# Output projection by seven products: another order of the products, product 1 in one part, weight loads spread over the tokens' terms

## The chip, the cores and the metric

The kernel runs on one core of a Trainium2 chip. The metric is the time of one execution on the device, in microseconds (us). A run is timed three times and the median is given. One more execution is taken by the hardware profiler; all rows below come from that one.

## The reference, cut to what matters

One block: a mixer (neighbourhood attention for half of the channels, a long convolution called Hyena for the other half), an output projection with a residual, then a mixture of 16 experts. The change is in the output projection only.

```python
mixed = jnp.concatenate([group_rms_norm(attn, attn_out_g[i], N_ATTN_HEADS),
                         group_rms_norm(hy, hyena_out_g[i], N_HYENA_GROUPS)], axis=-1)
x = x + jnp.einsum('bsd,de->bse', mixed, w_out[i])      # 1024 x 2048 by 2048 x 2048, float32
x = x + expert_choice_moe(rms_norm(x, ffn_norm_g[i]), w_router[i], w_gate[i], w_up[i], w_down[i])
```

## The kernel before, in words

**Stages.** The kernel first computes the input projection (tiles `pj`), woven with attention heads 0 to 5 and the filters, then the Hyena groups, then heads 6 and 7 (`attention`), then the output projection (`out_stream`, accumulators `o`), then for each token tile the router (`route`), then the top-k on VectorE and the experts (`pa`).

**Precision.** A float32 factor is split into a rounded part and a rest (`split`, L60 on ScalarE and L61 on VectorE; `wh` and `wl` for weights). One product of 128 x 128 by 128 x 512 is three matmuls (`mm3`, L68): rounded by rounded, rounded by rest, rest by rounded. The stationary operand is a piece of `s` (mixed tokens), the moving one is `wh` or `wl`.

**Seven products.** The projection is cut in halves three ways: tokens (512 each), channels (attention, Hyena) and columns. By the scheme of Strassen and Winograd, four blocks of the result come from seven products instead of eight. This is done twice, for `n` = 0 and 1, each with 2 x 512 columns. In `out_stream`, `where` names the four blocks of `w_out`: "11" and "12" belong to the attention channels, "21" and "22" to the Hyena channels. Each block is four loads of 512 KB (`load`, DRAM to tiles `b`). The sums of blocks are formed on VectorE (L943, L940, L946, L1015), and the generator `pairs` splits them; `wh` and `wl` have five buffers, and a product uses four of each. Products 2 and 4 need only Hyena outputs, product 1 only attention outputs, the others sums of both.

**Tokens' side.** `store_mixed` writes, for each head or group, rounded part and rest (`mxh`, `mxl`, one buffer each) of its combinations into seven DRAM arrays `sd`, one per product (L757): a head of the last two (6 and 7) writes five pairs, in the order 1, 5, 7, 6, 3. `fetch` reads 128 tokens of one array at a time, 1 MB, into `s` (two buffers).

**Jobs.** A job is one product and one quarter `t` of its 512 tokens: 8 channel blocks by 3 matmuls, 24 matmuls into one PSUM bank, in four parts `q` of 6. Before the change the order of products is 2, 1, 6, 4, 7, 5, 3. For `n` = 0 product 1 is cut in two: part 0 takes channel blocks 0 to 5 (heads 0 to 5), part 1 takes blocks 6 and 7 after both heads are mixed (the `yield lambda` on `self.mixed`). The four banks `o` stay open between them.

**What sets the order.** `weave` deals out generators by a modelled clock, so parts `q` fall between the pieces of head 7. A scheduler then fixes one order of instructions for each engine; engines work through it strictly in order, and SyncE (SP) issues nearly all DMAs from one such list. A DMA that has to wait therefore holds all DMAs behind it.

**Head 7.** For each of its eight query tiles j: scores `a` on TensorE, bias and maximum (`pe`, `ast`) on VectorE, exponential on ScalarE (L855), four or five transposes `t<-ident,pe`, a copy `pT` on ScalarE, and the product with the values (`t<-raw,pT`). Before tile 2, the second half of queries and keys is normalized (`raw`, L733) and transposed (`t<-ident,raw`).

Of the kernel before, what the change touches and what calls it, by code (L numbers as in the profile page):

```python
# [37 lines left out]
class Block:  # L38
# [862 lines left out]
    def out_stream(self, ctx):  # L901
# [12 lines left out]
        units = [(n, i) for n in range(2) for i in (2, 1, 6, 4, 7, 5, 3)]  # L914
# [3 lines left out]
        def load(n, name):  # L918
            c, k = where[name]
            B[n, name] = []  # L920
            for q in range(4):
                w = mp.tile([P, 2, 512], F32, name="b" + name, bufs=4)
                nc.sync.dma_start(w, a["w_out"][c + n, k + q])
                B[n, name].append(w)
# [8 lines left out]
        def pairs():  # L933
            for n, i in units:
                for q in range(4):
                    def b(x):
                        return B[n, x][q]

                    if i == 4:
                        tt(b("21"), b("21"), b("11"), op=ALU.add)  # L940
                    wh, wl, x = split(None if i == 6 else b({1: "11", 2: "21", 3: "22", 4: "21", 5: "11", 7: "12"}[i]))
                    if i == 6:
                        tt(x, b("22"), b("11"), op=ALU.subtract)  # L943
                    self.split(wh, wl, x)
                    if i == 1:
                        tt(b("11"), b("12"), b("11"), op=ALU.subtract)  # L946
                    W.append((wh, wl))
                    yield

        todo = pairs()  # L950
        jobs = [(n, i, t, part) for n, i in units
                for part in ((0, 1) if (n, i) == (0, 1) else (2,)) for t in range(4)]

        def fetch(j):

            if j < len(jobs):
                n, i, t, part = jobs[j]
                s = mp.tile([P, 2, NU, P], R, name="s", bufs=2)
                k = (slice(0, 6), slice(6, 8), slice(0, 8))[part]
                nc.sync.dma_start(s[:, :, k].bitcast(F32), self.sd[i][t, :, :, k])  # L960
                S.append(s)
# [6 lines left out]
        for name in ("21", "11", "12", "22"):  # L968
            load(0, name)
        fetch(0)  # L970
        for i in range(5):
            next(todo)
        yield
        sums, first, c11, c12, c21, now = {}, {}, {}, {}, {}, []
        for j, (n, i, t, part) in enumerate(jobs):
            if (n, i, t, part) == (0, 1, 0, 1):
                yield lambda: all(u in self.mixed for u in range(self.EARLY, NU))
                fetch(j)
            if j + 1 < len(jobs) and (*jobs[j + 1][:3], jobs[j + 1][3]) != (0, 1, 0, 1):
                fetch(j + 1)  # L980
            if t == 0 and part != 1:
                now = []
            if n == 0 and i in (7, 5, 3) and t == 1:
                load(1, {7: "21", 5: "12", 3: "11"}[i])
            if n == 1 and i == 2 and t == 0:
                load(1, "22")
# [8 lines left out]
            if part == 1:  # L995
                o = first[t]
            else:
                o = first[t] = self.po.tile([P, 512], F32, name="o", bufs=4)
            s = S.pop(0)
            for q in range(*{0: (0, 3), 1: (3, 4), 2: (0, 4)}[part]):  # L1000
# [7 lines left out]
                if t == 3:  # L1008
# [3 lines left out]
            if i in (1, 6) and part != 1 and t < 2:  # L1012
                for q in (2 * t, 2 * t + 1):
                    x, y = B[n, "21" if i == 1 else "12"][q], B[n, "22"][q]
                    tt(x, *((x, y) if i == 1 else (y, x)), op=ALU.subtract)  # L1015
            if part == 0:
                yield
                continue
# [402 lines left out]
```

## Time and profile before

| | us |
|---|---|
| median of 3 timed runs | 3318.38 (3318.09 to 3322.37) |
| the profiled execution, its own time | 3320.26 |
| its span, first to last instruction | 3318.5 |
| TensorE busy (page) | 3172.4, 96% of the span |
| output projection's first and last matmul starts | 1737.1 and 2162.1 |
| idle of TensorE just before matmuls into `o` whose rounded weights meet `s`, ended by the fetch of `s` | 30.0 |

The span is followed by stages: input projection and mixer to about 1737 us, output projection and router to 2166 us, top-k on VectorE to 2206 us, experts to the end. The granted clock of TensorE is given as a share of 2.4 GHz: 1.00 is 2.4 GHz, 0.50 is 1.2 GHz. A busy TensorE at 0.50 does half the work.

### The profile page before, as it was taken

The page shows a single profiled execution, that of the slowest core. Times are in us where ns is not written, and L with a number is a line of the kernel's source. Part 1 is how long each engine was busy: PE and PEld are TensorE (multiplying, and loading weights), DVE is VectorE, ACT ScalarE, POOL GpSimd, SP SyncE. Part 2 cuts the span into 40 slices and gives each one's busy share as a digit, 9 for nine tenths or more (in the row PEclk, how much of TensorE's full clock was granted, in tenths as well). Part 3 has the DMA queues.
Part 4 walks back from the last instruction along what each step waited for, and adds up shares of the span by engine and source line. Part 5 has one row for each costly group of instructions (what it writes and reads, how often), then busy time and mean ns, then how long its engine had stood idle before and what let it go on. Part 6 is the DMA issues. An engine that isn't in the chain of part 4 may idle for free.

```text
span 3318.5 us, 47116 instructions
## 1 busy us (share of the span) xinstructions
PE 3172.4 (96%) x17040; PEld 2761.8 (83%) x17040; DVE 2423.1 (73%) x3640; ACT 1854.0 (56%) x2883; POOL 84.9 (3%) x200
## 2 busy tenths in 40 slices
PE   8999999999999999999977899949999999999998
PEld 7899999998788888889975777838888888888887
DVE  5677776764567677667675355579999999899997
ACT  5455655543334334334353232448888888888886
POOL 0000000000000000000000000000000000000000
PEclk9999999999999999999988999979999999999999
DMA  7555555556666666765555886689999999999994
GB/s 248 191 168 169 175 187 189 173 172 207 200 222 207 201 209 213 226 216 175 181 213 179 297 288 215 229 337 339 404 403 386 405 404 403 401 389 405 403 404 136
DMA packets 313514, 876.82 MB, mean 264 GB/s; under 512 B 27173, under 2 KB 128720, under 8 KB 250049
## 3 DMA queue, kind: packets, MB, share of 16 engines
q1 hardware_dynamic: 307488, 837.26, 69.2%
q0 software_dynamic: 5648, 36.49, 4.2%
q8 instruction: 134, 2.20, 0.3%
q14 instruction: 100, 0.81, 0.1%
q10 hardware_dynamic: 144, 0.07, 0.0%
HBM read 781.07 MB, written 92.37 MB: 263 GB/s over the span
## 4 chain that ended last, share of the span: by engine, by line
PE 85%; DMA 7%; DVE 4%; issue 2%; ACT 1%; SPq 0%; POOLq 0%; POOL 0%; DVEq 0%; ACTq 0%
PE pa L68 29%; PE pj L68 29%; PE o L68 8%; PE c L68 5%; PE f L68 4%; DMA s<-sd 3%; PE a L68 3%; PE ct L79 2%; PE tp L1332 1%; DMA hl<-lo_d 1%; PE a L79 1%; PE ft L79 1%; DMA sd<-mxl 1%; PE t L79 1%; PE l L68 1%
## 5 line engine op out<-in xcount | busy, mean ns | idle before, releaser
L60 ACT CAST wh<-w 128x1024 fp32r<-128x1024 f32 (+2 forms) x1180 | 990.0, 846 | 595.9 <-PE pj L68 376.9
L61 DVE TENSOR_TENSOR wl<-w,wh 128x1024 fp32r<-128x1024 f32 (+2 forms) x1180 | 1122.3, 966 | 245.4 <-ACT wh L60 186.7
L68 PE MATMUL pa<-wh,xh 128*128 128x512 f32 x1024 | 400.3, 391 | 0.0
L68 PE MATMUL pa<-wh,xl 128*128 128x512 f32 x1024 | 398.6, 389 | 0.0
L68 PE MATMUL o<-wh,s 128*128 128x512 f32 x896 | 305.1, 409 | 30.1 <-DMA s<-sd 30.0
L68 PE MATMUL pj<-wh,hh 128*128 128x384 f32 x896 | 315.4, 352 | 2.9 <-ACT wh L60 2.9
L68 PE MATMUL pa<-wl,xh 128*128 128x512 f32 x1024 | 315.3, 389 | 0.0
L68 PE MATMUL pj<-hh,wh 128*128 128x512 f32 x768 | 314.7, 410 | 0.0
L68 PE MATMUL pj<-hl,wh 128*128 128x512 f32 x768 | 305.2, 397 | 8.9 <-DMA hl<-lo_d 8.9
L68 PE MATMUL pj<-wl,hh 128*128 128x384 f32 x896 | 305.3, 341 | 0.0
L68 PE MATMUL pj<-wh,hl 128*128 128x384 f32 x896 | 304.4, 340 | 0.0
L68 PE MATMUL pj<-hh,wl 128*128 128x512 f32 x768 | 302.8, 395 | 0.0
L68 PE MATMUL pa<-wh,el 128*128 128x512 f32 x1024 | 282.2, 397 | 0.2 <-DVE el L61 0.2
L68 PEld LDWEIGHTS o<-wh,s 128*128 128x128 f32 x896 | 173.0, 194 | 75.4 <-DMA s<-sd 34.5
L68 PEld LDWEIGHTS pa<-wl,xh 128*128 128x128 f32 x1024 | 192.2, 188 | 40.3
L68 PEld LDWEIGHTS pa<-wh,xh 128*128 128x128 f32 x1024 | 192.4, 188 | 39.4
L68 PEld LDWEIGHTS pa<-wh,xl 128*128 128x128 f32 x1024 | 192.3, 188 | 39.4
L68 PEld LDWEIGHTS pa<-wh,el 128*128 128x128 f32 x1024 | 187.2, 189 | 36.0 <-DVE el L61 0.7
L68 PE MATMUL o<-wl,s 128*128 128x512 f32 x448 | 180.6, 403 | 0.0
L68 PEld LDWEIGHTS pj<-wh,hh 128*128 128x128 f32 x896 | 169.6, 189 | 8.8 <-ACT wh L60 3.2
L68 PEld LDWEIGHTS pj<-hh,wl 128*128 128x128 f32 x768 | 144.6, 188 | 34.4
L68 PEld LDWEIGHTS pj<-wl,hh 128*128 128x128 f32 x896 | 169.9, 190 | 3.0 <-DVE raw L733 1.6
(329 smaller groups left out, 5544.3 us busy)
## 6 DMA issues: line engine op xcount, KB each, us to landing
hl<-lo_d SPq DMA_DIRECT2D x608, 256.0 KB, 3.1
w<-in_w_down_dram SPq DMA_DIRECT2D x128, 1024.0 KB, 11.9
w<-in_w_up_dram SPq DMA_DIRECT2D x127, 1024.0 KB, 10.4
w<-in_w_gate_dram SPq DMA_DIRECT2D x127, 1024.0 KB, 10.4
s<-sd SPq DMA_DIRECT2D x52, 1024.0 KB, 5.6
w<-in_w_at_dram SPq DMA_DIRECT2D x120, 384.0 KB, 3.5
w<-in_w_hy_dram SPq DMA_DIRECT2D x96, 256.0 KB, 3.6
Hd<-H SPq DMA_DIRECT2D x32, 513.0 KB, 4.1
```

What stands on the lines that cost most here:

```text
L60: nc.scalar.copy(hi, src)
L61: nc.vector.tensor_tensor(lo, src, hi.bitcast(F32), op=ALU.subtract)
L68: self.nc.tensor.matmul(out, w, x, start=start, stop=stop)
L79: self.nc.tensor.transpose(pt[:, i * P:(i + 1) * P], b, self.ident)
L1332: self.nc.tensor.transpose(pt[:, i * P:(i + 1) * P], src[:, c:c + (P - 1) * step + 1:step], self.ident)
```

## The change

The order of products becomes 2, 4, 1, 6, 7, 5, 3. Product 1 is one part again and starts, as a whole, after heads 6 and 7 are mixed; products 2 and 4 stand before that wait. The block sums follow the new order: "21" is first reduced by "22" and increased by "12" (after the first two token quarters of product 2, L1011 after), then reduced by "11" when product 4's weights are made (L938). Loads of blocks are spread: for `n` = 0, "21" comes first, then "22", "12" and "11" at product 2's first three quarters; for `n` = 1 one 512 KB load per token quarter, at products 1, 7, 5 and 3. The preparation of the next product's weights starts one step earlier, at the end of quarter 2.

```diff
-        units = [(n, i) for n in range(2) for i in (2, 1, 6, 4, 7, 5, 3)]
+        units = [(n, i) for n in range(2) for i in (2, 4, 1, 6, 7, 5, 3)]
...
-        def load(n, name):
+        def load(n, name, q):
             c, k = where[name]
-            B[n, name] = []
-            for q in range(4):
-                w = mp.tile([P, 2, 512], F32, name="b" + name, bufs=4)
-                nc.sync.dma_start(w, a["w_out"][c + n, k + q])
-                B[n, name].append(w)
+            w = mp.tile([P, 2, 512], F32, name="b" + name, bufs=4)
+            nc.sync.dma_start(w, a["w_out"][c + n, k + q])
+            B.setdefault((n, name), []).append(w)
...
                     if i == 4:
-                        tt(b("21"), b("21"), b("11"), op=ALU.add)
+                        tt(b("21"), b("21"), b("11"), op=ALU.subtract)
...
+                        if q == 0:
+                            tt(b("11"), b("12"), b("11"), op=ALU.subtract)
                         tt(x, b("22"), b("11"), op=ALU.subtract)
                     self.split(wh, wl, x)
-                    if i == 1:
-                        tt(b("11"), b("12"), b("11"), op=ALU.subtract)
...
-        jobs = [(n, i, t, part) for n, i in units
-                for part in ((0, 1) if (n, i) == (0, 1) else (2,)) for t in range(4)]
+        jobs = [(n, i, t) for n, i in units for t in range(4)]
+        late = (0, 1, 0)
...
-        for name in ("21", "11", "12", "22"):
-            load(0, name)
+        for q in range(4):
+            load(0, "21", q)
         fetch(0)
-        for i in range(5):
+        for i in range(4):
             next(todo)
...
-            if (n, i, t, part) == (0, 1, 0, 1):
+            if (n, i, t) == late:
                 yield lambda: all(u in self.mixed for u in range(self.EARLY, NU))
...
-            if n == 0 and i in (7, 5, 3) and t == 1:
-                load(1, {7: "21", 5: "12", 3: "11"}[i])
-            if n == 1 and i == 2 and t == 0:
-                load(1, "22")
+            if n == 0 and i == 2 and t < 3:
+                for q in range(4):
+                    load(0, ("22", "12", "11")[t], q)
+            elif n == 0 and i in (1, 7, 5, 3):
+                load(1, {1: "21", 7: "12", 5: "11", 3: "22"}[i], t)
...
-                if t == 3:
+                if q == 3 if t == 2 else t == 3 and q < 3:
                     next(todo, None)
...
+            if i == 2 and t < 2:
+                for q in range(4):
+                    x = B[n, "21"][q]
+                    tt(x, x, B[n, ("22", "12")[t]][q], op=(ALU.subtract, ALU.add)[t])
+            if i == 1 and t == 2:
+                for q in range(1, 4):
+                    x = B[n, "11"][q]
+                    tt(x, B[n, "12"][q], x, op=ALU.subtract)
```

**Where the instructions stand.** On TensorE, at the first matmul into `o`: before, the scores of head 7's first tiles (`a`), their transposes (`pe`) and the transposes of its second half (`raw`) come first.

```order
L68 MATMUL a<-qkh_19216,qkh_19214 128x288
L68 MATMUL a<-qkl_19217,qkh_19214 128x288
L68 MATMUL a<-qkh_19216,qkl_19215 128x288
L79 MATMUL t<-ident,pe 128x128 x4
L79 MATMUL t<-ident,raw 128x128 x8
L68 MATMUL o<-wh,s 128x512
L68 MATMUL o<-wl,s 128x512
```

After, at the first matmul into `o` on TensorE (the `mxo` are head 6's first output half, the `raw` head 7's first half):

```order
L68 MATMUL pj_18539<-wh,hl 128x384
L79 MATMUL t<-ident,pe 128x128 x4
L68 MATMUL t<-raw,pT 128x128 x4
L79 MATMUL t<-ident,mxo 128x128 x4
L79 MATMUL t<-ident,raw 128x128 x8
L68 MATMUL o<-wh,s 128x512
L68 MATMUL o<-wl,s 128x512
```

The first two quarters of product 2 (48 matmuls) have moved ahead of head 7's scores; the third and fourth quarter and product 4 are dealt out between head 7's pieces. In the new order, 24 matmuls of product 4 (its first quarter) stand between head 7's tiles 1 and 2, and the other 72 between the pieces of tiles 2 to 5.

On SP, after head 7's bias table `T`: before, all 16 loads of `w_out` come ahead of the first fetch of `s`; after, four.

```order
 L815 DMA T<-in_rpb_t_dram 128x1536
+L921 DMA b_19104<-in_w_out_dram 128x1024
+L921 DMA b_19106<-in_w_out_dram 128x1024
+L921 DMA b_19108<-in_w_out_dram 128x1024
+L921 DMA b_19110<-in_w_out_dram 128x1024
+L957 DMA s<-sd_61 128x2048 x2
+L921 DMA b_19132<-in_w_out_dram 128x1024
```

```order
-L923 DMA b_19130<-in_w_out_dram 128x1024
-L923 DMA b_19132<-in_w_out_dram 128x1024
-L923 DMA b_19134<-in_w_out_dram 128x1024
-L960 DMA s<-sd_61 128x2048 x2
-L965 DMA x_19161<-in_x_dram 128x512
```

The other 12 loads have moved: four stand behind the fetches of product 2's first two quarters, four behind the third's, four behind the fourth's.

On SP, where head 7's mixed output is stored (`sd_60` is product 1's array) and product 1 begins. Before:

```order
L1070 DMA w_22405<-in_w_up_dram 128x2048
L757 DMA sd_60<-mxh 128x4x128
L757 DMA sd_60<-mxl 128x4x128
L1070 DMA w_22407<-in_w_gate_dram 128x2048
L757 DMA sd_64<-mxh 128x4x128
L757 DMA sd_64<-mxl 128x4x128
L960 DMA s<-sd_60 128x2x256 x2
```

After:

```order
L1071 DMA w_22405<-in_w_up_dram 128x2048
L757 DMA sd_60<-mxh 128x4x128
L757 DMA sd_60<-mxl 128x4x128
L1071 DMA w_22407<-in_w_gate_dram 128x2048
L957 DMA s<-sd_60 128x2048
L757 DMA sd_64<-mxh 128x4x128
L757 DMA sd_64<-mxl 128x4x128
L957 DMA s<-sd_60 128x2048
```

The first fetch of product 1 stands one pair of stores earlier, and each fetch there is 1 MB instead of 256 KB.

On VectorE, before product 4's weights in the new order (head 7's `qkl` are its second half; `mxl` and `mxo` are head 6's stores):

```order
L739 SCALAR_TENSOR_TENSOR qkl_19200<-t,qkg,qkh_19199 128x512
L856 RECIPROCAL ast<-ast 128x1
L853 TENSOR_TENSOR pe<-a,T 128x288
L938 TENSOR_TENSOR b_19104<-b_19104,b_19306 128x1024
L938 TENSOR_TENSOR b_19106<-b_19106,b_19308 128x1024
L61 TENSOR_TENSOR wl<-b_19104,wh 128x1024
L938 TENSOR_TENSOR b_19108<-b_19108,b_19310 128x1024
```

Before the change the rows behind the same `qkl` are:

```order
L739 SCALAR_TENSOR_TENSOR qkl_19217<-t,qkg,qkh_19216 128x512
L1015 TENSOR_TENSOR b_19120<-b_19128,b_19120 128x1024
L1020 TENSOR_TENSOR x_19161<-o,x_19161 128x512
L61 TENSOR_TENSOR mxl<-mxp,mxh 128x512
```

Product 4's sums and splits (four L938, four L61) have come in here, behind the load of "11" and among head 7's tiles.

## Rows read from the trace of the kernel before

**Rows 1.** The page, 40 slices of the span (82.96 us each), busy and clock tenths.

```profile
PE   8999999999999999999977899949999999999998
...
PEclk9999999999999999999988999979999999999999
```

**Rows 2.** Busy time of each engine by stage; first line names the columns.

```profile
core 0: us, PE busy (x) PEld busy (x) DVE busy (x) ACT busy (x) POOL busy (x), PEclk, DMA share, GB/s
1713.00:1737.00 24.00, 9.05 (x34) 7.04 (x35) 23.63 (x36) 14.98 (x24) 0.00 (x0) 0.59 1.03 406
1737.00:1764.00 27.00, 26.29 (x106) 20.67 (x105) 12.11 (x14) 6.49 (x10) 0.00 (x0) 0.92 0.64 204
1764.00:1802.00 38.00, 33.49 (x206) 28.33 (x205) 31.18 (x55) 17.76 (x29) 0.80 (x4) 1.00 0.27 92
1802.00:1826.00 24.00, 7.43 (x21) 4.58 (x19) 8.56 (x14) 7.63 (x12) 1.06 (x2) 0.59 0.79 257
...
1836.50:1868.70 32.20, 29.70 (x137) 24.05 (x138) 7.46 (x14) 4.31 (x8) 0.00 (x0) 0.89 0.76 273
1868.70:1891.20 22.50, 22.50 (x101) 18.64 (x100) 8.45 (x10) 4.63 (x6) 0.00 (x0) 1.00 0.86 326
1891.20:2162.50 271.30, 262.47 (x1290) 214.78 (x1288) 141.90 (x220) 92.99 (x154) 0.00 (x0) 0.99 0.72 245
```

**Rows 3.** Chain of work that ended last: start us, duration us, what.

```profile
1737.45 7.40 PE o L68 x24
1744.87 5.62 DMA s<-sd
...
1771.65 0.89 PE t L68 x8
...
1813.27 8.22 DMA sd<-mxh
...
2052.36 35.66 PE o L68 x156
```

**Rows 4.** TensorE in order of time: start us, us, instruction [idle before <-releaser].

```profile
1713.65 0.66 PE L79 MATMUL t<-ident,raw 128*128 128x128 f32 x4 [1.59 <-ACT mx L770]
...
1735.69 1.75 PE L79 MATMUL t<-ident,raw 128*128 128x128 f32 x7 [5.75 <-DVE raw L733]
...
1763.91 1.05 PE L68 MATMUL t<-raw,pT 128*128 128x128 f32 x8
...
1800.87 1.16 PE L68 MATMUL t<-raw,pT 128*128 128x128 f32 x8 [0.75 <-ACT pT L863]
...
1815.68 0.80 PE L68 MATMUL o<-wh,s 128*128 128x512 f32 x1 [7.60 <-DMA s<-sd]
...
1836.51 0.47 PE L68 MATMUL o<-wh,s 128*128 128x512 f32 x1 [3.36 <-DMA s<-sd]
```

**Rows 5.** SyncE's DMA issues in order of time, same columns.

```profile
1704.41 14.35 SPq L923 DMA_DIRECT2D b<-in_w_out_dram  x16
...
1805.05 0.38 SPq L757 DMA_DIRECT2D sd<-mxl  x1
```

**Rows 6.** ScalarE in order of time, same columns.

```profile
1711.98 1.03 ACT L60 CAST wh<-b 128x1024 fp32r<-128x1024 f32 x1
...
1752.73 0.62 ACT L60 CAST mxh<-mxo 128x512 fp32r<-128x512 f32 x1 [14.05 <-DMA sd<-mxh]
1757.20 0.62 ACT L60 CAST mxh<-mx 128x512 fp32r<-128x512 f32 x1 [3.85 <-DMA sd<-mxh]
...
1821.56 0.62 ACT L60 CAST mxh<-mx 128x512 fp32r<-128x512 f32 x1 [8.32 <-DMA sd<-mxh]
```

**Rows 7.** VectorE by line, 1713 to 1802 us: xcount | busy us, mean ns.

```profile
L61 DVE TENSOR_TENSOR wl<-b,wh 128x1024 fp32r<-128x1024 f32 x12 | 14.5, 1218 | 1.1 <-ACT wh L60 1.1
L1015 DVE TENSOR_TENSOR b<-b,b 128x1024 f32<-128x1024 f32 x8 | 9.6, 1212 | 0.0
```

**Rows 8.** TensorE's waits, 1891 to 2165 us: us in total, times, longest.

```profile
PE o L68 <- DMA s<-sd: 8.7, 10, 1.6
```

More of the change, by code (lines that the diff above doesn't have):

```diff
@@ L950, in out_stream @@
         todo = pairs()
-        jobs = [(n, i, t, part) for n, i in units
-                for part in ((0, 1) if (n, i) == (0, 1) else (2,)) for t in range(4)]
+        jobs = [(n, i, t) for n, i in units for t in range(4)]
+        late = (0, 1, 0)
         def fetch(j):
             if j < len(jobs):
-                n, i, t, part = jobs[j]
+                n, i, t = jobs[j]
                 s = mp.tile([P, 2, NU, P], R, name="s", bufs=2)
-                k = (slice(0, 6), slice(6, 8), slice(0, 8))[part]
-                nc.sync.dma_start(s[:, :, k].bitcast(F32), self.sd[i][t, :, :, k])
+                nc.sync.dma_start(s.bitcast(F32), self.sd[i][t])
                 S.append(s)
@@ L966, in x_of @@
             return x
-        for name in ("21", "11", "12", "22"):
-            load(0, name)
+        for q in range(4):
+            load(0, "21", q)
         fetch(0)
-        for i in range(5):
+        for i in range(4):
             next(todo)
         yield
-        sums, first, c11, c12, c21, now = {}, {}, {}, {}, {}, []
-        for j, (n, i, t, part) in enumerate(jobs):
-            if (n, i, t, part) == (0, 1, 0, 1):
+        sums, c11, c12, c21, now = {}, {}, {}, {}, []
+        for j, (n, i, t) in enumerate(jobs):
+            if (n, i, t) == late:
                 yield lambda: all(u in self.mixed for u in range(self.EARLY, NU))
                 fetch(j)
-            if j + 1 < len(jobs) and (*jobs[j + 1][:3], jobs[j + 1][3]) != (0, 1, 0, 1):
+            if j + 1 < len(jobs) and jobs[j + 1] != late:
                 fetch(j + 1)
-            if t == 0 and part != 1:
+            if t == 0:
                 now = []
-            if n == 0 and i in (7, 5, 3) and t == 1:
-                load(1, {7: "21", 5: "12", 3: "11"}[i])
-            if n == 1 and i == 2 and t == 0:
-                load(1, "22")
+            if n == 0 and i == 2 and t < 3:
[3 more added lines that the diff above has]
+                load(1, {1: "21", 7: "12", 5: "11", 3: "22"}[i], t)
             if i == 2:
@@ L994, in out_stream @@
                 c22 = x_of(t + 4, 2 + n)
[L995 to L998, printed above, removed]
+            o = self.po.tile([P, 512], F32, name="o", bufs=4)
             s = S.pop(0)
-            for q in range(*{0: (0, 3), 1: (3, 4), 2: (0, 4)}[part]):
+            for q in range(4):
                 if t == 0:
@@ L1011, in out_stream @@
                     yield
-            if i in (1, 6) and part != 1 and t < 2:
-                for q in (2 * t, 2 * t + 1):
[L1014 to L1018, printed above, removed]
+            if i == 2 and t < 2:
+                for q in range(4):
+                    x = B[n, "21"][q]
[4 more added lines that the diff above has]
+                    tt(x, B[n, "12"][q], x, op=ALU.subtract)
+            if i == 6 and t < 2:
+                for q in (2 * t, 2 * t + 1):
+                    x = B[n, "12"][q]
+                    tt(x, B[n, "22"][q], x, op=ALU.subtract)
             if i in (2, 1):
```

## The prediction, made before the changed kernel ran

> **What bounds the kernel now.** I read four views in this order. The page's slices come first: TensorE is at 9 or more in nearly all of them, and falls only in slices 21 to 23 and in slice 27, the top-k [rows 1]. A change in the projection is therefore worth what it takes out of the hole at slices 21 to 23, or of the smaller losses behind it. The windows by stage split that hole [rows 2]. From 1713 to 1737 us TensorE is busy 9.05 of 24 us, at a granted clock of 0.59, while VectorE is busy 23.63: there VectorE is the bound. From 1764 to 1802 head 7 and product 1's part 0 run together. From 1802 to 1826 nearly everything waits: TensorE 7.43 of 24. From 1868.7 on TensorE is full: 22.5 of 22.5 us, then 262.47 of 271.3. TensorE's own order says what ends each hole [rows 4]: the transposes of head 7's second half are done only at 1735.69, held 5.75 us by `raw` on VectorE, and every matmul of the projection stands behind them. Head 7's last values start at 1800.87 and last 1.16 (X = 1802.0); then TensorE waits 7.60 us for the fetch of `s`, and product 1's rest starts at 1815.68. The chain of work shows the stores of head 7 on the way there, 8.22 us in one piece [rows 3]. Product 6 starts at 1836.51 [rows 4], X + 34.5.
>
> So before product 6, 132 us after the loads of `w_out` begin at 1704.41 [rows 5], only products 2 and 1 are done: 192 matmuls. At full clock one costs 35.66/156 = 0.229 us [rows 3], which makes 44 us.
>
> **Term 1, head 7 ends earlier.** Four loads of 512 KB and the first fetch of 1 MB now come behind the 0.75 MB table: 3.9 MB, at the 406 GB/s of that stretch [rows 2] 9.7 us, so `s` is there at about 1714.6. The first weight cast ran at 1711.98 [rows 6] and stays. TensorE's rows ahead of the first matmul into `o` now end with transposes that started at 1713.65 [rows 4]. Product 2 starts at about 1715.5 instead of 1737. Its first quarter takes 7.4 us, as the one after a pause did [rows 3], the second 24 x 0.229 = 5.5: 1728.4. The third, with head 7's scores in between, and the eight transposes take it to about 1739.5; the fourth ends at 1745.
>
> Product 4 needs "11", which is asked for last. From the release of the first `s` buffer (1722.9) SP has 7.3 MB to move up to there: two fetches, eight loads, two inputs of 256 KB, one pair of stores. At 406 GB/s that is 18 us: 1741. VectorE then has four sums and four splits, 8 x 1.22 = 9.7 us [rows 7], and about 2.5 us of other rows among them. It gets there behind head 7's second half, at 1745, and ends at 1757; the last six matmuls of product 4's first quarter end at 1758.4. From there head 7 needs what it needed from the end of tile 1's values (1771.65 + 0.89 [rows 3]) to X, 29.5 us, and 5.5 for 24 matmuls more than stood among them before: 1793.4. One thing is new: head 6's four later pairs of stores now fall among head 7's tiles, and ScalarE, in whose queue head 7's exponentials and copies stand, waits for the one `mxh` buffer. Before it waited 14.05, 3.85 and 8.32 us at such casts [rows 6], with nothing urgent behind. Bounds for the four: 0 to 4 x 8.3 = 33 us; I take 2.5 in all, nearest to the 3.85, most of it beside product 4. X' = 1795.9, **6.1 us gained**.
>
> A page of the Trainium skill speaks against this term: DMA: Bandwidth & Descriptors, Specifications, gives about 358 GB/s as what HBM gives one core. By that the 7.3 MB take 20.4 us and the sum below loses 2.4. The row shows 406 GB/s, and the row decides.
>
> **Term 2, product 1 in one part.** Before, X to product 6 took 34.5 us with 24 matmuls; now 96. The first fetch stands one pair of stores earlier (behind the `mxl` at 1805.05 [rows 5]) but brings 1 MB: first matmul at X' + 12.5, for 13.7 before. First quarter 7.4, second 5.5: X' + 25.4. The third fetch stands behind stores 2 to 4, each of which waits for the one before; store 4 was cast at 1821.56 [rows 6], X + 19.6, and again I add the quarter's own traffic: issue at X' + 22, landing after 5.6 us [rows 3]. The third quarter then runs from X' + 27.5 to 33, the fourth, behind store 5 and the first output, from 33 to 38.5. Product 6 starts at X' + 39: **4.5 us lost**. Bounds: X' + 33 if no fetch stalls (1.5 gained), X' + 59 if each does (below).
>
> The same page of the Trainium skill, under Anatomy of one DMA, gives 2.0 us plus bytes at 436 GB/s, 4.4 for 1 MB. By that the two late fetches save 2.4 us together. Rows 3 show 5.62 for one in this stage, with other traffic around it.
>
> **Term 3, product 4 leaves the full stretch.** 96 x 0.229 = 22 us; the window in which it ran, 1868.7 to 1891.2, is 22.5 with TensorE busy throughout [rows 2]. **22 us gained.** TensorE's matmuls are the same 1344 in all; the term is real only because they now fill the hole.
>
> **Term 4, loads of 512 KB one per quarter.** Behind product 4, waits for `s` cost 8.7 us in ten pieces of at most 1.6 [rows 8]. Loads side by side with the fetch are one cause, output and router writes others, and those stay. From 0 to 8.7; I take **3 us gained**.
>
> **Edits at nothing.** VectorE gets four more sums per column half, 4 x 1.21 us [rows 7]. For `n` = 0 they stand where it waits for blocks anyway, for `n` = 1 in a stretch in which it is busy 141.9 of 271.3 us [rows 2]; without that cover they cost up to 9.7. Weights made one step earlier hide behind a quarter of 5.5 us. Four banks no longer stay open; nothing waited for them. The next stage moves as it is: its loads wait for the projection's memory.
>
> **Sum.** 6.1 - 4.5 + 22 + 3 = 26.6 us. The profiled execution took 3320.3 with a span of 3318.5; 3293.7 for it. The median of the runs is 1.9 lower: **3292**.
>
> **Rivals.** A measurement of this kernel tells a difference from none at about 0.2%, 6.6 us.
>
> *Head 7 is not earlier.* VectorE, full from 1713 to 1737, keeps its sums for product 2 (eight, now ahead of tile 0's maximum) and could hold head 7 as before: X' = X. For: 31.18 of 38 us busy from 1764 to 1802 [rows 2]. Against: the rows up to X are about as many as before, and TensorE waits for none of them in its first 48 matmuls. Gain 20.5: 3298.
>
> *Stores pace product 1.* Each of its three later fetches waits out a pair of stores of 8.2 us and then lands in 5.6 [rows 3]: 13.8 us a quarter, product 6 at X' + 12.5 + 41.4 + 5.5 = X' + 59, 20 more than above. Gain 6.6: 3312, on the bound of what can be told. For: those rows. Against: by the third fetch most of head 7's pairs are out, and the first two fetches stand ahead of them.
>
> *Slower: ScalarE held by head 6's stores.* The four later pairs stand on ScalarE ahead of head 7's exponentials and copies; if each cast waits 11 us, between the 8.32 and the 14.05 [rows 6], head 7 ends 44 us later instead of 2.5. It decides from (26.6 + 6.6 + 2.5)/4 = 8.9 us a cast. Then 3318.4 - 26.6 + 41.5 = 3333. For: those rows. Against: the pairs now come between product 4's fetches, when DMA has little else to do (92 GB/s from 1764 to 1802 [rows 2]).
>
> *No effect.* The early products only move the hole, since product 1 still waits for both heads and all `w_out` for its order: within 3312 to 3325. It needs X' some 20 us late; the matmuls ahead of head 7 are 48 + 24 + 24 = 96, as many as product 2's were before, and start 21 us sooner.
>
> **How the numbers follow.** Forecast 0.62, head 7 not earlier 0.16, stores pace product 1 0.10, ScalarE held 0.08, no effect 0.04. Faster by over 0.2%: 0.62 + 0.16 and half of the second rival, 0.83; within 0.2%: the other half and no effect, 0.09; slower: 0.08. The range goes up to 3313, over the second rival, and leaves out the last two (0.12). Downward: head 7 at 1786 if "11" is split as it lands (10 more), product 6 at X' + 35 (4), all 8.7 of the waits (5.7) make 19.7: 3272, not all at once; I take 3274.
>
> **What would show it.** First matmul into `o` near 1715; product 2 done by 1745; product 4's first quarter done near 1758; head 7's last values near 1795; product 6 near 1835; last matmul into `o` near 2136 instead of 2162, and the experts' stage as long as before. Wrong if head 7's last values come after 1802, if ScalarE's `mxh` casts among its tiles wait over 5 us each, if product 1 takes over 35 us, or if VectorE's splits hold TensorE at product 4 of the second column half.

## The result, and the profile after

The changed kernel takes 3293.3 us (median of four runs, 3290.3 to 3295.3); beside it the kernel before took 3319.8. The ratio is 0.9919, with a 95% interval of 0.9902 to 0.9936: 27 us faster (21 to 33). The forecast was 3292, in a range of 3274 to 3313. Direction and time came out; two of the four terms did not, as the profile shows. One of the six timed runs of the kernel with product 1 in two parts (below) took 5936.3 us at a granted clock of 0.834, for 0.983 to 0.986 in its other five, and is left out of its median and ratio.

The profiled execution of the changed kernel took 3295.3 us, with a span of 3293.5. The page's slices first, which answer [rows 1]:

```profile
PE   8999999999999999999997999949999999999998
...
PEclk9999999999999999999998999979999999999999
```

Slices 21 to 23 had 7, 7 and 8 tenths before; now only slice 22 has 7. The windows by stage answer [rows 2]; columns are busy us of each engine with the number of instructions, then granted clock, DMA share and GB/s:

```profile
core 0: us, PE busy (x) PEld busy (x) DVE busy (x) ACT busy (x) POOL busy (x), PEclk, DMA share, GB/s
1708.00:1732.00 24.00, 21.84 (x92) 17.49 (x92) 22.01 (x29) 10.32 (x15) 0.00 (x0) 0.86 0.93 348
1732.00:1755.00 23.00, 17.11 (x91) 13.94 (x91) 21.35 (x33) 11.50 (x18) 0.40 (x2) 0.98 0.91 317
1755.00:1790.10 35.10, 32.45 (x180) 27.64 (x181) 25.18 (x46) 15.43 (x25) 0.40 (x2) 0.92 0.49 177
1790.10:1817.00 26.90, 14.64 (x59) 11.68 (x58) 12.73 (x18) 6.55 (x11) 1.06 (x2) 0.75 0.85 275
1817.00:1833.00 16.00, 11.92 (x52) 9.25 (x52) 4.41 (x6) 5.65 (x12) 0.00 (x0) 0.89 0.90 314
1833.00:1866.00 33.00, 31.21 (x151) 25.02 (x151) 17.09 (x23) 9.58 (x12) 0.00 (x0) 1.00 0.83 284
```

The first row is the hole that the change aimed at: TensorE is busy 21.84 of 24 us there, for 9.05 before, while VectorE is as full as it was. The hole behind head 7 is still there (14.64 of 26.9). TensorE in order of time, which answers [rows 4]; columns are start, duration, instruction and, in brackets, the idle time before it and what ended it:

```profile
1710.80 0.79 PE L68 MATMUL o<-wh,s 128*128 128x512 f32 x1 [1.56 <-DMA s<-sd]
...
1754.91 0.79 PE L68 MATMUL o<-wh,s 128*128 128x512 f32 x1 [3.16 <-DMA s<-sd]
...
1804.32 0.79 PE L68 MATMUL o<-wh,s 128*128 128x512 f32 x1 [5.58 <-DMA s<-sd]
...
1821.44 0.50 PE L68 MATMUL o<-wh,s 128*128 128x512 f32 x1 [4.01 <-DMA s<-sd]
...
1839.33 0.50 PE L68 MATMUL o<-wh,s 128*128 128x512 f32 x1 [0.25 <-DMA s<-sd]
```

The rows are the starts of product 2, of product 4's second quarter, of product 1, of its third quarter and of product 6. Head 7's last values end at 1790.5.

One thing has to be taken off first. The last bias table `T`, ahead of every moved instruction, is asked for at 1704.02 in the trace before and at 1698.94 in the trace after: 5.1 of the 25.0 us between the two spans were there before the change could act. So stages are counted from that load, here called T0. X is the end of head 7's last values, as in the prediction.

| from T0, us | before | after |
|---|---|---|
| first matmul into `o` | 33.1 | 11.9 |
| X | 98.0 | 91.6 |
| product 6 starts | 132.5 = X + 34.5 | 140.4 = X + 48.8 |
| product 7 starts | 187.2, behind products 6 and 4 | 165.6, behind product 6 |
| last matmul into `o` starts | 458.1 | 438.3 |
| from there to the end of the span | 1156.4 | 1156.3 |

The stage gained 19.8 us, and what follows it is unchanged. The prediction's signs: its times for product 2 and for head 7 came, product 6 is late (X + 48.8 for 39), and of its signs of being wrong one lies on the edge: product 1 takes 35.0 us, 1804.32 to 1839.33, where "over 35" was named.

### The profile page after: what moved, and what is told of

Its sections match the earlier page's. It is cut to its first block, busy times and chain, and to the rows that moved or that the text cites. A ratio compares the mean times of both kernels' runs of the same rounds, so it can differ in the third digit from the quotient of the medians.

```text
span 3293.5 us, 47095 instructions
## 1 busy us (share of the span) xinstructions
PE 3164.4 (96%) x17040; PEld 2756.7 (84%) x17040; DVE 2432.1 (74%) x3648; ACT 1851.8 (56%) x2881; POOL 85.1 (3%) x200
## 4 chain that ended last, share of the span: by engine, by line
PE 83%; DMA 9%; DVE 3%; issue 3%; ACT 1%; SPq 0%; POOLq 0%; POOL 0%; DVEq 0%; ACTq 0%
PE pa L68 30%; PE pj L68 29%; PE o L68 6%; PE c L68 5%; PE f L68 4%; DMA s<-sd 3%; PE a L68 3%; PE ct L79 2%; PE tp L1333 1%; DMA hl<-lo_d 1%; DMA sd<-mxl 1%; PE a L79 1%; PE ft L79 1%; DMA w<-in_w_down_dram 1%; PE t L79 1%
## 5 line engine op out<-in xcount | busy, mean ns | idle before, releaser
L61 DVE TENSOR_TENSOR wl<-w,wh 128x1024 fp32r<-128x1024 f32 (+2 forms) x1180 | 1122.5, 966 | 243.4 <-ACT wh L60 183.7
L68 PEld LDWEIGHTS o<-wh,s 128*128 128x128 f32 x896 | 172.4, 193 | 68.9 <-DMA s<-sd 32.8
L68 PEld LDWEIGHTS pa<-wh,el 128*128 128x128 f32 x1024 | 187.2, 189 | 36.0 <-DVE el L61 0.7
## 6 DMA issues: line engine op xcount, KB each, us to landing
w<-in_w_down_dram SPq DMA_DIRECT2D x128, 1024.0 KB, 11.8
w<-in_w_up_dram SPq DMA_DIRECT2D x127, 1024.0 KB, 10.4
```

The source lines that it names most:

```text
L61: nc.vector.tensor_tensor(lo, src, hi.bitcast(F32), op=ALU.subtract)
L68: self.nc.tensor.matmul(out, w, x, start=start, stop=stop)
```

## The experiments

"Stage" is the time from T0 to the start of the last matmul into `o`. Medians are of the timed runs; ratios are to the kernel before, timed beside them (medians 3317.7 to 3321.6).

| run | median us | ratio, 95% interval | T0 | X - T0 | stage |
|---|---|---|---|---|---|
| before, again | 3325.5 (one run) | | 1702.4 | 99.7 | 464.2 |
| after, again | 3294.4 | 0.9928, 0.9905 to 0.9950 | 1701.2 | 91.8 | 438.0 |
| after, third | 3295.7 | 0.9926, 0.9909 to 0.9944 | 1697.8 | 91.5 | 436.8 |
| early loads alone | 3307.3 | 0.9969, 0.9959 to 0.9980 | 1701.6 | 88.0 | 442.5 |
| order alone | 3307.9 | 0.9964, 0.9945 to 0.9982 | 1703.4 | 99.8 | 446.7 |
| product 1 in two parts | 3293.0 | 0.9926, 0.9905 to 0.9947 | 1706.3 | 96.6 | 442.8 |
| loads by four again | 3296.0 | 0.9929, 0.9905 to 0.9952 | 1699.3 | 90.4 | 437.3 |
| expert loads held | 3292.6 | 0.9916, 0.9895 to 0.9936 | 1698.2 | 90.9 | 436.9 |
| fetches by GpSimd | 3299.7 | 0.9938, 0.9918 to 0.9959 | 1699.8 | 92.9 | 439.8 |
| three buffers `s` | 3278.8 | 0.9879, 0.9861 to 0.9898 | 1704.0 | 90.4 | 415.3 |
| three buffers, expert loads held | 3271.1 | 0.9860, 0.9838 to 0.9883 | 1698.2 | 89.8 | 414.7 |
| the same, product 1 filled in | 3274.5 | 0.9858, 0.9839 to 0.9876 | 1698.1 | 90.2 | 420.3 |

### Scatter or change: both kernels again

No edit.

> The kernel before, unchanged, once more. In the two traces the load of the last bias table `T` is issued at 1704.02 us before and at 1698.95 after, although every engine has the same instructions in the same order up to there. Theory A, scatter between executions: this repeat issues it anywhere from 1698 to 1705. Theory B, it belongs to the kernel: 1703 to 1705 again. From that load to the last matmul into `o` both expect 458 us, as in the first trace (1704.02 to 2162.1).

> The kernel after, unchanged, once more. Theory A, scatter: the load of the last `T` is issued anywhere from 1698 to 1705, and the median of the timed runs stays between 3290 and 3300. Theory B, it belongs to the kernel: 1698 to 1700, and again 3290 to 3295. From that load to the last matmul into `o` both expect 438 us (1698.95 to 2137.2), 20 less than before; product 2 starts 17 us behind the load.

> The kernel after once more, beside the two runs with three buffers `s`. Expected as before: 3293 (3290 to 3297), 438 us from the load of `T` to the last matmul into `o`, and the load of `T` anywhere from 1698 to 1706 us.

SyncE's issue of the last table in the repeat of before and in the first one of after (in the kernel with product 1 in two parts it comes at 1706.26):

```profile
1702.37 0.33 SPq L815 DMA_DIRECT2D T<-in_rpb_t_dram  x1
```

```profile
1701.20 0.33 SPq L815 DMA_DIRECT2D T<-in_rpb_t_dram  x1
```

Product 2 starts 12.1 and 12.0 us behind T0 in the two repeats of after, not 17 as expected. Over all traces T0 lies between 1697.8 and 1706.3, with no relation to the kernel that shows: the 5.1 us are scatter, and theory A holds. The repeat of before had a stage of 464.2, 6 us longer than its first trace, so one pair of traces is not exact for the stage either. Means of two and three traces give 461.2 - 437.7 = 23.5 us, and the three timed comparisons 0.9919, 0.9928 and 0.9926, which is 24 to 27 us.

### The early loads alone, the order alone

The old order of products with "21" loaded first (`early_old`; shown against the kernel before), and the rest of the change, the new order above all, with all sixteen loads first (`front16`; against the kernel after; called "order alone" here, though product 1 is one part in it too and the later loads are spread):

```diff
-        for name in ("21", "11", "12", "22"):
-            load(0, name)
+        load(0, "21")
...
+            if n == 0 and i == 2 and t < 3:
+                load(0, ("11", "12", "22")[t])
```

> The early loads alone: block 21 first, then the fetch, the other blocks at product 2's first three quarters, but the old order of products (2, 1, 6, 4, ...), product 1 in two parts and the loads of the second column half as before. My theory: the early start lets product 2 fill the hole at 1713 to 1737, but without product 4 ahead of head 7 there are only 72 matmuls of product 1's part 0 to follow it; head 7 ends about 6 us earlier, everything behind it stays as long as before, product 4 stays in the full stretch: 3312 (3306 to 3316). Rival, the early start is the whole gain: 3290 to 3298. Rival, the order is all and the start nothing: within 3318 to 3322.

```diff
-        for q in range(4):
-            load(0, "21", q)
+        for name in ("21", "22", "12", "11"):
+            for q in range(4):
+                load(0, name, q)
...
-            if n == 0 and i == 2 and t < 3:
-                for q in range(4):
-                    load(0, ("22", "12", "11")[t], q)
-            elif n == 0 and i in (1, 7, 5, 3):
+            if n == 0 and i in (1, 7, 5, 3):
```

> The kernel after with all 16 loads of the first column half ahead of the first fetch, as the kernel before has them: the new order without the early start. My theory: 8.4 MB and the first fetch come before product 2, which starts some 26 us behind the load of `T` instead of 12; head 7 ends near 103 us behind that load (91.6 after, 98 before), and what stands behind head 7 is as after. Gain over before some 9 us of 25: 3310 (3304 to 3315). Rival, the order of products is the whole gain: 3290 to 3298. Rival, without the early start the order is worth nothing: 3317 to 3322.

TensorE with the early loads alone: first matmul into `o`, head 7's last values, and product 6:

```profile
1713.49 0.50 PE L68 MATMUL o<-wh,s 128*128 128x512 f32 x1 [1.65 <-DMA s<-sd]
...
1787.55 2.04 PE L68 MATMUL t<-raw,pT 128*128 128x128 f32 x8 [0.88 <-DVE on L877]
...
1823.90 0.77 PE L68 MATMUL o<-wh,s 128*128 128x512 f32 x1 [4.65 <-DMA s<-sd]
```

and with the order alone, first matmul into `o` and head 7's last values:

```profile
1734.77 0.78 PE L68 MATMUL o<-wh,s 128*128 128x512 f32 x1
...
1802.02 1.16 PE L68 MATMUL t<-raw,pT 128*128 128x128 f32 x8 [0.75 <-ACT pT L863]
```

The early loads alone start product 2 at T0 + 11.9 and end head 7 at T0 + 88.0, 10 us earlier than before (6 were expected); product 6 still comes X + 34.3, as before it. The order alone starts product 2 at T0 + 31.3 and leaves head 7 where it was (99.8; 26 and 103 were expected), and yet gains: product 4 is no longer in the full stretch. By the ratios the one is worth 10 us (7 to 14) and the other 12 (6 to 18); both together 24 to 27. The two halves of the change add up within their intervals, and neither is the whole. In the complete change head 7 ends 3.6 us later than with the early loads alone. The likely reason, not shown by a run of its own, is that 24 matmuls more stand ahead of it there, as many as product 4's first quarter.

### Product 1 in two parts again

```diff
+        jobs = [(n, i, t, part) for n, i in units
+                for part in ((0, 1) if (n, i) == (0, 1) else (2,)) for t in range(4)]
+        late = (0, 1, 0, 1)
...
+                k = (slice(0, 6), slice(6, 8), slice(0, 8))[part]
+                nc.sync.dma_start(s[:, :, k].bitcast(F32), self.sd[i][t, :, :, k])
```

> The kernel after with product 1 in two parts again: channel blocks 0 to 5 ahead of head 7's end, blocks 6 and 7 behind it. My theory: the 72 matmuls of part 0 take 16.5 us, and from 1755 to 1790 us TensorE is busy 32.45 of 35.1 us in the kernel after, so head 7 ends some 14 us later; behind it product 6 starts 34.5 us on, as before, instead of 48.8. The two cancel: 3293 (3288 to 3298). Rival, one part is what made the gain possible: 3302 or more. Rival, the 14.3 us that one part lost behind head 7 come back: 3279 to 3284.

TensorE, first matmul of part 1 and product 6:

```profile
1817.33 0.79 PE L68 MATMUL o<-wh,s 128*128 128x512 f32 x1 [5.33 <-DMA s<-sd]
...
1840.35 0.77 PE L68 MATMUL o<-wh,s 128*128 128x512 f32 x1 [3.94 <-DMA s<-sd]
```

Head 7 ended 5 us later (14 expected), product 6 came 37.5 us behind it instead of 48.8, and the times cannot be told apart (0.9926 here, 0.9919 to 0.9928 after). The stage of its one trace is 4.5 to 6 us longer than after's three. That product 1 is one part gained or lost nothing that the times can tell.

### Loads of the second half by four again

```diff
-                load(1, {1: "21", 7: "12", 5: "11", 3: "22"}[i], t)
+                if t == 1:
+                    for q in range(4):
+                        load(1, {1: "21", 7: "12", 5: "11", 3: "22"}[i], q)
```

> The kernel after with the second column half's loads as four at once, at the second quarter of products 1, 7, 5 and 3, instead of one a quarter. In the traces the stretch from product 6 on took 272.8 us after and, less product 4's 22.5, 270.9 before, so the spread seems worth nothing. My theory now: from the load of `T` to the last matmul into `o` 438 us as after, 3294 (3290 to 3297). The prediction's term 4: 3 us slower than after, 3297, up to 8.7, 3303.

The stage is 437.3 us, between the traces of after (436.8 to 438.3). Spreading these loads is worth nothing that this trace or the times show; the prediction's 3 us were wrong.

### What holds product 1: the queue, the traffic, the buffers

First the chain of work of the kernel after, from head 7's last values on (start, duration, what):

```profile
1789.68 1.14 DVE b L1015
...
1791.08 1.13 DVE b L943
...
1793.50 2.27 DVE b L1019 x2
...
1801.62 4.17 DMA sd<-mxl
...
1806.60 7.89 DMA sd<-mxl
...
1815.77 5.63 DMA s<-sd
```

The fetch of the third quarter, at 1815.77, stands behind two pairs of stores that took 4.17 and 7.89 us. On SyncE:

```profile
1790.54 0.33 SPq L1071 DMA_DIRECT2D w<-in_w_up_dram  x1
1792.72 0.38 SPq L757 DMA_DIRECT2D sd<-mxh  x1
...
1793.96 0.66 SPq L1071 DMA_DIRECT2D w<-in_w_gate_dram  x1
1797.52 0.33 SPq L957 DMA_DIRECT2D s<-sd  x1
...
1815.77 0.50 SPq L957 DMA_DIRECT2D s<-sd  x1
```

Two loads of expert weights, 1 MB each, are in front of the first fetch. Queue order and traffic are two explanations of the same rows. The fetches moved to GpSimd's queue (`pool_f`), and the two expert loads held until the fourth token tile's first output (`exp_late2`):

```diff
-                nc.sync.dma_start(s.bitcast(F32), self.sd[i][t])
+                (nc.gpsimd if (n, i) == (0, 1) else nc.sync).dma_start(s.bitcast(F32), self.sd[i][t])
```

> The kernel after with product 1's four fetches issued by GpSimd instead of SyncE, so that they wait for their own buffer and data but no longer behind the stores of head 7 in SyncE's queue. Theory B, queue order: the third quarter's wait (4.0 us) and the half clock behind it go, product 6 starts 42 to 45 us behind head 7's last values instead of 48.8: 3289 (3285 to 3291). Theory A, traffic: the fetch starts earlier and lands as late, product 6 at 47 to 50: 3294. Against both: GpSimd's loads of the router's weights now stand behind the fetches, and the routers may hold VectorE: 3298 or more.

```diff
+        if (t, c) == (3, 0):
+            self.rd = rd
...
-        with tc.issue_after(self.first_cast.ins), tc.issue_after(self.first_sub.ins):
+        with tc.issue_after(self.first_cast.ins), tc.issue_after(self.first_sub.ins), \
+                tc.issue_after(self.rd.ins):
```

> The kernel after, but the two loads of expert weights of 1 MB that are issued at 1790.5 and 1794.0 us, just ahead of head 7's first stores and product 1's first fetch, are held behind the first output of the fourth token tile. Theory A, traffic: with 2 MB less the first pair of stores and the first fetch land about 4 us sooner and the next pairs too; product 6 starts 40 to 43 us behind head 7's last values instead of 48.8: 3287 (3284 to 3290). Theory B, the stall is the order of the queue and the wait for one buffer at each store, not traffic: product 6 still 47 to 50 us behind, 3294.

GpSimd's fetch of the third quarter, then TensorE's first matmul on it:

```profile
1814.76 0.53 POOL L957 DMA_DIRECT2D s<-sd  x1 [13.58 <-PE o L68]
```

```profile
1823.43 0.50 PE L68 MATMUL o<-wh,s 128*128 128x512 f32 x1 [3.54 <-DMA s<-sd]
```

With X at 1792.8, this fetch is issued at X + 22.0 for X + 25.3 in the kernel after, released by TensorE alone. TensorE has it 8.7 us later instead of 5.7, and the quarter starts at X + 30.7 for 30.9. Product 6 starts at X + 49.7, within theory A's 47 to 50. The queue's order is not what costs here: theory B falls. That GpSimd's queue by itself is slower is not what the first fetch shows, 7.1 us from issue to the matmul for 6.8 on SyncE; but head 7's third pair of stores went out later in this run too (X + 18.9 for 15.3). The time, 3299.7, is in the range of "against both", but its interval overlaps after's. With the expert loads held (X at 1789.1), first the landing of the first stores and of the first fetch in the chain of work, then TensorE's first matmul of product 1:

```profile
1792.12 2.39 DMA sd<-mxl
...
1794.64 4.81 DMA s<-sd
```

```profile
1799.50 0.80 PE L68 MATMUL o<-wh,s 128*128 128x512 f32 x1 [2.17 <-DMA s<-sd]
```

The first stores are issued 2.2 us behind X in both kernels, so it is the landings that differ. Product 1 starts at X + 10.4 instead of 13.8, its third quarter at X + 23.8 instead of 30.9, product 6 at X + 37 instead of 48.8 (theory A: 40 to 43; the router's matmuls, here behind product 6's start, are a part of this), and product 7 at T0 + 158.9 for 165.6, 168.2 and 167.0 in the three traces of after: traffic is what costs, as theory A says. But the time that theory A gave, 3287, did not come (3292.6): the stage ends at 436.9, at the lower end of after's 436.8 to 438.3. TensorE's waits from product 7 on (us in total, times, longest), first with the expert loads held, then after:

```profile
PE o L68 <- DMA s<-sd: 15.0, 17, 3.0
```

```profile
PE o L68 <- DMA s<-sd: 8.9, 13, 2.6
```

What was gained was given back there: the stretch from product 7 on takes 278.0 us, for 272.7, 269.8 and 269.8 in the three traces of after, whose waits are 8.9, 10.4 and 9.7.

### Three buffers for `s`

The waits behind product 6 might then have a cause of their own. Both kernels fetch one quarter ahead, into two buffers. Three fit if the weights have four pairs of buffers instead of five:

```diff
-            wh = wo.tile([P, 2, 512], R, name="wh", bufs=5)
-            wl = wo.tile([P, 2, 512], R, name="wl", bufs=5)
+            wh = wo.tile([P, 2, 512], R, name="wh", bufs=4)
+            wl = wo.tile([P, 2, 512], R, name="wl", bufs=4)
...
-                s = mp.tile([P, 2, NU, P], R, name="s", bufs=2)
+                s = mp.tile([P, 2, NU, P], R, name="s", bufs=3)
...
-            if j + 1 < len(jobs) and jobs[j + 1] != late:
-                fetch(j + 1)
+            while f < min(j + 3, len(jobs) if j >= jobs.index(late) else jobs.index(late)):
+                fetch(f)
+                f += 1
...
-                if q == 3 if t == 2 else t == 3 and q < 3:
+                if t == 3:
```

> The kernel after with three buffers `s` instead of two, so that a fetch is issued two quarters ahead; the memory for it comes from `wh` and `wl`, four buffers instead of five, and the next product's weights are split in the last quarter, as in the kernel before. Theory: what the waits for `s` cost behind product 6 (8.5 us after, 8.7 before) comes from having only one fetch ahead; they shrink to under 3 us, and product 1's third fetch no longer waits for its first quarter to end: from the load of `T` to the last matmul into `o` 428 to 432 us instead of 438, 3285 to 3289. Rival: with four weight buffers TensorE waits for `wl` at each of the thirteen next products, 0.5 to 1 us each, which takes the gain away: 3291 to 3298.

> As the run with three buffers `s`, and the two loads of expert weights held behind the first output of the fourth token tile as well. Theory: holding the loads alone brought product 7 forward by 6.5 us or more, of which 1.3 us were left at the last matmul into `o`, since waits for `s` behind it grew (11.4 us up to the end of product 2 of the second half, 5.5 us after); with a fetch more ahead these waits go, and the two gains add: 422 to 428 us, 3280 to 3285. Rival: the transfers of this stretch are what bounds it, and the waits only move: 432 to 438 us, 3289 to 3295.

Matmuls into `o` by line, of the kernel after (count | busy us, mean ns | idle before, what ended it):

```profile
L68 PE MATMUL o<-wh,s 128*128 128x512 f32 x896 | 305.3, 409 | 25.5 <-DMA s<-sd 24.3 <-DVE wl L61 1.1
```

and with three buffers and the expert loads held, with the window from product 7 on there and, last, with three buffers alone:

```profile
L68 PE MATMUL o<-wh,s 128*128 128x512 f32 x896 | 295.8, 402 | 6.6 <-DMA s<-sd 6.2 <-ACT wh L60 0.5
```

```profile
1853.70:2113.00 259.30, 257.36 (x1286) 213.36 (x1284) 147.59 (x226) 93.06 (x155) 0.00 (x0) 1.00 0.78 271
```

```profile
1861.90:2119.40 257.50, 257.20 (x1287) 213.61 (x1285) 146.95 (x226) 93.27 (x155) 0.00 (x0) 1.00 0.76 262
```

From product 7 on TensorE no longer waits for `s` at all in either, and the stretch takes 257.5 and 259.3 us for 272.7, 269.8 and 269.8 in the three traces of after. The wait for weights that the rival expected is 0.3 us there. With three buffers the kernel takes 3278.8 us; with the expert loads held as well, 3271.1, which is 1.4% under the kernel before and 0.7% under the change; 3285 to 3289 and 3280 to 3285 were expected, so both gained more than the theory says. Of the 22 us by which the stage is shorter with three buffers alone (415.3 for a mean of 437.7), 9 come ahead of product 7 (T0 + 158 for 167) and 13 behind it. In the traces the two stages differ by 0.6 us only (415.3 and 414.7), so what holding the loads adds there stays open: the timed runs say 8 us, but their intervals overlap, and 6 us of the difference between the two profiled executions is T0.

Last, product 1's first six channel blocks placed around and behind head 7's end in that kernel:

```diff
+        late, held = jobs.index((0, 1, 0, 0)), jobs.index((0, 1, 0, 1))
...
+            while f < min(j + 3, len(jobs) if j > late else held):
+                fetch(f)
+                f += 1
+            if j == late:
+                yield lambda: all(u in self.mixed for u in range(self.EARLY, NU))
```

> The run with three buffers `s` and the expert loads held, and product 1 in two parts again, but the first part (channel blocks 0 to 5, 72 matmuls, 16.5 us) not ahead of head 7's end, where TensorE is full: its fetches are ahead, its matmuls come last in the program's order there and so stand around and behind head 7's last values, while the stores and the fetches of blocks 6 and 7 run. Theory: what is lost at product 1 is the wait from head 7's last values to its first matmul, 10.8 us with three buffers; the first part fills it, product 6 starts 23 to 28 us behind head 7's last values instead of 34.8, and the last matmul into `o` comes 405 us behind the load of `T` instead of 415: 3261 (3257 to 3267). Rival: the second part, 24 matmuls, is paced by the five pairs of stores as in the kernel before, where product 6 came 34.5 us behind head 7's last values with no more than these 24 between: 3271 again.

TensorE, first matmul of the second part and first matmul of product 6:

```profile
1810.96 0.80 PE L68 MATMUL o<-wh,s 128*128 128x512 f32 x1 [5.66 <-DMA s<-sd]
...
1826.09 0.77 PE L68 MATMUL o<-wh,s 128*128 128x512 f32 x1 [12.21 <-DMA s<-sd]
```

Product 1 is done at 1813.9, X + 25.6, as the theory says; then TensorE waits 12.2 us for product 6's first fetch and starts it at X + 37.8. The theory's 3261 did not come; the rival's 3271 came nearer, for another reason: not part 1 but product 6 is held. Product 6 needs the array that the fourth pair of head 7's stores writes, and in all kernels where little stands between it comes no sooner: X + 34.5 before, 37.5 with product 1 in two parts, 37 with the loads held and two or three buffers (product 1 whole), 37.8 here. With the loads held, product 1 whole fits into that time, and cutting it brought nothing. Why the stage is 5.6 us longer here (420.3 for 414.7), though product 6 starts only 1.2 us later from T0, stays open.

## Why the prediction was right, and where it was not

**Term 1, head 7 ends earlier: right.** Predicted from T0: first matmul into `o` 11.5, product 4's first quarter done 54.4, X 91.9. Measured: 11.9, 52.5, 91.6. The gain is 6.4 us for 6.1. The prediction says that by the Trainium skill's 358 GB/s (DMA: Bandwidth & Descriptors, Specifications) the sum would lose 2.4 us. By its own steps it would lose nothing: "11" would be there at 1743.4 instead of 1741, and VectorE comes to it only at 1745. The stretch in question of the kernel after moved 334 GB/s, nearer to the 358 than to the row's 406 (columns as above):

```profile
1718.00:1738.00 20.00, 17.54 (x90) 14.24 (x90) 19.12 (x29) 6.53 (x12) 0.00 (x0) 1.00 0.92 334
```

The first `s` too was there later than by 406 GB/s, 11.8 us behind T0 for 10.6. Even so VectorE's first sum with "11" (L938, 1738.16) waited for no load. VectorE went from row to row up to it, so its order paced that step, as the prediction had it, and not the rate. ScalarE's four casts for head 6's later stores waited 0, 0, 0 and 4.91 us, 2.5 in all forecast:

```profile
1755.69 0.62 ACT L60 CAST mxh<-mxp 128x512 fp32r<-128x512 f32 x1 [4.91 <-DMA sd<-mxh]
```

The rival that priced them at 11 us each did not come. `early_old` shows that the early loads are the cause: they moved X by themselves.

**Term 2, product 1 in one part: mis-sized.** Predicted 4.5 us lost between X and product 6, measured 14.3 (48.8 - 34.5). The first matmul came at X + 13.8 for 12.5, the third quarter at 30.9 for 27.5, and from there to product 6 were 17.9 us for 11.5. Three things failed. The third fetch was put at X + 22 behind stores 2 to 4 and given 5.6 us to land; it was issued at 25.3, since pair 3's buffer was free only after 7.89 us, and in GpSimd's run an earlier issue landed no earlier. The 4.4 us for 1 MB that the prediction cites from the Trainium skill (DMA: Bandwidth & Descriptors, Anatomy of one DMA) stands there for DMAs issued from GpSimd. GpSimd's third fetch took 8.7 us here, SyncE's 5.7. And the quarters were priced at full clock but for the first; behind the two waits they ran at 0.85 and 0.83 (windows of the kernel after, columns as above):

```profile
1804.50:1817.50 13.00, 12.93 (x48) 10.18 (x48) 1.99 (x3) 2.45 (x4) 0.00 (x0) 0.85 0.82 257
1817.50:1827.50 10.00, 6.06 (x20) 4.86 (x21) 1.29 (x2) 2.03 (x5) 0.00 (x0) 0.83 1.02 346
```

Third, router work was not counted: four groups of the router's matmuls stood in product 6 before, and now three of them stand ahead of it, in and behind product 1's last quarter. The last of the three, a quarter of a microsecond ahead of product 6:

```profile
1838.01 1.07 PE L68 MATMUL l<-wr,xt 128*128 128x16 f32 x8 [0.26 <-ACT xt L1121]
```

Against that stands a term that was not in the sum: product 6 took 25.1 us instead of 32.2, without these three groups and at a clock of 1.00 instead of 0.89 [rows 2]. So part of the loss is work that only changed its place. The net is 7.2 lost. In the repeats of after product 6 starts at X + 48.4 and 48.0 and takes 28.0 and 27.5 us, in that of before X + 34.7 and 32.8.

**Term 3, product 4 out of the full stretch: right.** 22 predicted; its window of 22.5 us (26.3 in the repeat of before) is gone, and its matmuls now lie between T0 + 47 and T0 + 83. `front16` shows that the gain does not hang on the early start.

**Term 4, loads one per quarter: wrong in its mechanism.** Predicted 3 gained; the stretch from product 7 on took 272.7 for 270.9, and TensorE waited 8.9 us in 13 pieces for 8.7 in ten [rows 8]; the repeats, 269.8 and 269.8 for 270.6, show no gain beyond a microsecond either. `burst1` gives the same stage with loads by four. The runs with three buffers show what the waits were: with one fetch ahead there were 8.9 us of them, with two none.

**Edits at nothing: nearly.** VectorE's sums, priced at nothing, stand in the chain above (L1015, L943, L1019), between the steps of head 7's mix. Head 7's second half is transposed at X + 7.1 for X + 4.9 before, 2.2 us later; that the sums alone are the reason was not tried. The bound given was 9.7.

**The sum.** 6.4 - 14.3 + 7.1 + 22.5 - 1.9 = 19.8 us in the pair of traces, for 26.6 predicted; over all traces 23.5. That the time was met to 1.3 us is partly luck: terms 2 and 4 came out 9.8 and 4.9 us worse than forecast, 7.1 of that was made up by product 6, which no term held, and 5.1 in the two profiled executions by scatter ahead of T0. Of the rivals, stores pacing product 1 came nearest: X + 48.8 lies midway between the forecast's 39 and its 59. One fetch, the third, waited behind stores as it says, not each of three.

## What to carry to other kernels

Where one engine waits because another is full, move work into that place that needs the waiting engine and little of the full one, and see that it comes out of a stretch that is full: the two halves were worth 10 and 12 us here, each without the other. Where waits of up to 3 us lie spread over a long stretch, try first how far ahead a transfer is issued: here one more buffer made the kernel 17 us faster (3278.8 us beside 3295.7), where moving loads in time, with two buffers, gave nothing that could be told. A transfer issued 3.3 us earlier into nearly full DMA was used no earlier here (X + 30.7 for 30.9), and with 2 MB less beside it 7 us earlier: look at the traffic before reordering a queue.

## What the runs showed of the hardware

A wait can cost more than its length. In the kernel after, TensorE from 2036 us on (start, duration, instruction):

```profile
2036.20 0.50 PE L68 MATMUL o<-wh,s 128*128 128x512 f32 x1 [2.58 <-DMA s<-sd]
...
2037.67 1.05 PE L68 MATMUL o<-wh,s 128*128 128x512 f32 x2
...
2042.91 0.62 PE L68 MATMUL o<-wh,s 128*128 128x512 f32 x2
```

```profile
2036.20:2040.00 3.80, 3.80 (x11) 3.04 (x12) 0.38 (x1) 0.00 (x0) 0.00 (x0) 0.63 0.30 92
```

Behind a wait of 2.58 us two matmuls take 1.05 us instead of 0.62 for a while, as at the lower of the clock's two levels (1.2 and 2.4 GHz); the granted clock of the first 3.8 us is 0.63. In the three traces of after the waits from product 7 on are 8.9, 10.4 and 9.7 us and the stretch 272.7, 269.8 and 269.8; the two kernels with three buffers, which differ in more than the waits, have 0 and 0.3 and 257.5 and 259.3. In the means that is 12.4 us shorter for 9.5 us of waits less.

DMA can be nearly full at less throughput: in the 14 us behind X its engines are busy 0.91 of the time at 300 GB/s, where [rows 2] have 1.03 at 406. The window of the kernel after, and the packets of each of the two stretches, after first:

```profile
1790.50:1804.50 14.00, 1.74 (x10) 1.10 (x8) 10.35 (x15) 4.60 (x7) 1.06 (x2) 0.66 0.91 300
```

```profile
DMA packets 2374, 4.20 MB, mean 300 GB/s; under 512 B 102, under 2 KB 1979, under 8 KB 1979
```

```profile
DMA packets 3573, 9.73 MB, mean 406 GB/s; under 512 B 310, under 2 KB 1334, under 8 KB 3316
```

With head 7's stores in it five packets in six are under 2 KB, without them three in eight. That the size of the packets is the cause was not tried.

And the same instructions in the same order reach T0 anywhere between 1697.8 and 1706.3 us: 8.5 us of scatter ahead of the stage over fourteen traces, a third of the whole effect.
